# A bfloat16 column for the output tiles' scale, and ScalarE's square ahead of VectorE's product in the last tile

## The chip, the cores and the metric

The kernel runs on one core of a Trainium2 chip. The metric is the device time of one execution in microseconds (us), the median of several runs. The engines are named as in the profile: PE is TensorE (PEld its weight loads), DVE is VectorE, ACT is ScalarE, POOL is GpSimd, SP is SyncE, whose queue issues the transfers spoken of here.

## The reference

One decoder layer: a sequence of 2048 rows of 1024 features goes through two attention mixers (8 heads each, 64 wide), whose outputs are gated, put side by side, multiplied with the output weights, normalised and added to the input.

```python
def reference(x, c, positions, w_ada, b_ada, g_pre, w_in, b_fgate, sinks, w_out, g_post):
    ...
        h = rms_norm(x, g_pre[l]) * (1.0 + scale[:, None, :]) + shift[:, None, :]
        proj = h @ w_in[l]
        ...
        oa = oa * jax.nn.silu(za)
        ...
        ob = ob * jax.nn.silu(zb)
        y = jnp.concatenate([oa, ob], axis=-1) @ w_out[l]
        x = x + gate[:, None, :] * rms_norm(y, g_post[l])
```

`rms_norm(y, g)` divides each row by the root of its mean square (plus 1e-6) and multiplies by `g`. The change lies in the last two of these lines.

## The kernel before

All products run on PE in 16-bit floats: each f32 operand is scaled by a power of two or a similar factor into float16 range and split into a high and a low half, and a product is the sum of three matmuls (high by high, high by low, low by high). The program runs in stages: weights and input, the input projection with the sliding-window mixer, the forgetting attention (to about 1000 us), and then the output product, whose first tiles are mixed into the end of the attention.

**The output stage** goes over 16 tiles of 128 rows (class `Out`, `t` from 0 to 15). A tile passes these steps:

- `load`: SP's queue brings the attention outputs (`oT`, by transposing transfers, L1483; for the first four tiles `o`) and the gate path `z` (L1485).
- `turn`: the outputs are multiplied with `z` on DVE (`gate`, L1502 in tiles 0 to 3, L1505 and L1506 after them). ACT squares the product and sums along each row (`squares_`, L1510), which leaves one f32 number on each of the 128 partitions, the tile `gs` (shown as `w_mx`). `scale_` sums those 128 numbers over the partitions and gives every partition the sum: one PE matmul of the 128x128 matrix of ones (stationary) with the column `gs` (moving), L1514, into a PSUM column `pg`. `root_scale` (DVE, L128 and L129) makes from its bits an approximate reciprocal root `sc`, which scales the tile into float16 range; DVE also forms `inv`, with which the scale is taken out again later (L1518, L1519). ACT writes the high half of the scaled tile (`hi`, L1524), DVE the low half (`lo`, L1525); both make up `hl`, shown as `oz`.
- `product`: 48 matmuls over two halves of 512 output columns (L1576): per half, 8 units `k` of 3 matmuls each with 128x128 weights from `oz` and 512 columns of the output weights `wohl`. At the end of a half, DVE multiplies the PSUM result with `inv` and the gate row into `y` (L1585, shown as `hT`), and ACT squares the same PSUM result and sums it into `ss` (L1586, writes `sv`). `root` makes the reciprocal root of the mean square (L1596, then the small instructions L101 to L119), `store` the final multiply and add (L1605) and the transfer out (L1606).
- In the last tile (`t` = 15) the second half goes through `last`: two quarters of 256 columns (`h` = 0 and 1, 24 matmuls each, L1540), each with a product on DVE (L1547) and a square on ACT (L1548) of its own, so that after the very last matmul only a quarter's work is left. After `h` = 1 comes the reciprocal root on DVE (L103 to L119), then the final multiply and add in two halves (L1605), each followed by its transfer.

**What sets the order.** The stage is written out by hand: `ofill` calls the product units one after another, with the table `oev` naming the unit before which a tile's `load` or `turn` is called (`turn` of tile t comes 22 units before its first product). Work is put off by `after(n, f)`: `f` runs n ticks later; from tile 4 on a tick comes every second unit. `turn(5)` thus runs `gate` after 1 tick, the squares after 2, `scale_` after 5, `hi` after 6 and `lo` after 7. The instruction of `scale_` therefore sits between two product units of an earlier tile on PE's queue. Each engine takes its instructions in the order in which they were written, and waits on semaphores for those of other engines that wrote or read the same tile before.

Of the kernel before, what the change touches and what calls it, by code (L numbers as in the profile page):

```python
# [12 lines left out]
BF16 = mybir.dt.bfloat16  # L13
I16 = mybir.dt.int16
I32 = mybir.dt.int32
AF = mybir.ActivationFunctionType
# [27 lines left out]
def hybrid_layer(  # L44
# [17 lines left out]
    V, A, G, PE, SP = nc.vector, nc.scalar, nc.gpsimd, nc.tensor, nc.sync  # L62
# [20 lines left out]
    def sm(n, tag):  # L83
        return small.tile([P, n], F32, tag=tag, name=tag)
# [12 lines left out]
    def rsqrt_parts(dst, ss, n, more=None, eng=None):  # L97
        W = eng or V
        v = sm(n, "rs_v")
        if more is None:  # L100
            V.tensor_scalar(v[:], ss, 1.0 / D, EPS, op0=ALU.mult, op1=ALU.add)  # L101
        else:
            V.scalar_tensor_tensor(v[:], ss, 1.0 / D, more, op0=ALU.mult, op1=ALU.add)  # L103
        y = sm(n, "rs_y")
        h = small.tile([P, n], I32, tag="rs_h", name="rs_h")
        V.tensor_scalar(h[:], v[:].bitcast(I32), 1, None, op0=ALU.logical_shift_right)  # L106
        V.tensor_scalar(y[:].bitcast(I32), h[:], -1, 0x5F3759DF, op0=ALU.mult, op1=ALU.add)  # L107
        W.tensor_scalar(v[:], v[:], -0.5, None, op0=ALU.mult)
        for it in range(3):
            yield  # L110
            t = sm(n, "rs_t")
            if n == 1:
                W.scalar_tensor_tensor(t[:], y[:], y[:], v[:], op0=ALU.mult, op1=ALU.mult)  # L113
            else:
                W.tensor_tensor(t[:], y[:], y[:], op=ALU.mult)
                W.tensor_tensor(t[:], t[:], v[:], op=ALU.mult)
            y2 = dst if it == 2 else sm(n, "rs_y")
            if eng is None:
                V.scalar_tensor_tensor(y2[:], t[:], 1.5, y[:], op0=ALU.add, op1=ALU.mult)  # L119
            else:  # L120
                W.tensor_scalar(t[:], t[:], 1.5, None, op0=ALU.add)
                W.tensor_tensor(y2[:], t[:], y[:], op=ALU.mult)
            y = y2

    def root_scale(dst, ss):

        h = small.tile([P, 1], I32, tag="rs_h", name="sc_h")
        V.tensor_scalar(h[:], ss.bitcast(I32), 1, None, op0=ALU.logical_shift_right)  # L128
        V.tensor_scalar(dst.bitcast(I32), h[:], -1, 0x5F3759DF + (15 << 23), op0=ALU.mult, op1=ALU.add)  # L129
# [35 lines left out]
    ones = const.tile([P, P], F32, name="ones")  # L165
# [20 lines left out]
    def bank(hold=False):  # L186
        n = next(n for n in order_ if n not in held)
        order_.remove(n)
        order_.append(n)
        if hold:  # L190
            held.add(n)
        return n

    def release(n):
        held.discard(n)
        order_.remove(n)
        order_.append(n)
# [4 lines left out]
    def after(n, f):  # L202
        late.append([n, f])
# [227 lines left out]
    def turn(ci, k, px=None):  # L431

        px = px or ps_x.tile([P, CH], F32, tag="x", name="px")
        for u in range(4):
            PE.transpose(px[:, u * P:(u + 1) * P], xt[ci * 4 + u][:, k * P:(k + 1) * P], ident[:])
        hf = hst.tile([P, CH], F32, tag="hf", name="hf")
        hi, lo = hT[ci][:, 0, k, :], hT[ci][:, 1, k, :]

        def scaled():
            for dst in ([hi] if k % 2 == 0 else []) + [hf[:]]:  # L440
                A.activation(dst, px[:], AF.Identity, scale=Gp[:, k:k + 1], bias=Shp[:, k:k + 1])

        def split():
            if k % 2:
                V.tensor_copy(hi, hf[:])
            V.tensor_tensor(lo, hf[:], hi, op=ALU.subtract)

        return scaled, split

    def turn_x(ci, k):  # L450
        scaled, split = turn(ci, k)
        after(1, scaled)
        after(2, split)
# [9 lines left out]
    start = ExitStack()  # L463
    st = start.enter_context(tc.tile_pool(name="start", bufs=1, reuse_waits="tile"))
    wad = start.enter_context(tc.tile_pool(name="wad", bufs=8, reuse_waits="tile"))
    with tc.manual_schedule():
# [172 lines left out]
        w_low("kb", 0, 1)  # L639
        w_low("vb", 0, 1)  # L640
        turned = [turn(0, k) for k in range(5)]
        squares(1)
        shf0 = col8("shf0")
# [9 lines left out]

        PE.transpose(bk[0][0:1, 0:P], bmx[:], ident[:])
        turned += [turn(0, k, bk[k - 4]) for k in (5, 6)]
        bm = st.tile([1, 1], F32, name="bm")
        V.tensor_reduce(bm[:], bk[0][0:1, 0:P], axis=AX.X, op=ALU.max)
# [749 lines left out]
    def w_slot(n):  # L1407
        return oio["w"][:, n // KT, n % KT, :]
# [26 lines left out]
    def xy(n):  # L1435

        return hT[2][:, n // 2, 4 * (n % 2):4 * (n % 2) + 4, :].rearrange("p k n -> p (k n)").bitcast(F32)
# [24 lines left out]
    class Out:  # L1462
# [24 lines left out]
        def turn(self, lag):  # L1487

            if self.t < 4:
                px = [bk[bank()][:].rearrange("p (k n) -> p k n", k=4) for _ in range(2)]  # L1490
                for k in range(KT):
                    PE.transpose(px[k // 4][:, k % 4, :], self.o[:, k * P:(k + 1) * P], ident[:])
            self.hl = wpool.tile([P, 2, KT, P], F16, tag=("whl", "wraw")[self.t % 2], name="oz")
            self.sc = sm(1, "w_pw")
            hi, lo = self.hl[:, 0], self.hl[:, 1]
            gs = sm(1, "w_mx")

            def gate():
                if self.t < 4:
                    for h in range(2):  # L1500
                        z = self.z[:, 4 * h:4 * h + 4, :]
                        V.tensor_tensor(z, px[h], z, op=ALU.mult)  # L1502
                    return
                of = ozp.tile([P, KT, P], F32, tag="of", name="of")
                V.tensor_tensor(of[:], self.oT[:, 0], self.oT[:, 1], op=ALU.add)  # L1505
                V.tensor_tensor(self.z, of[:], self.z, op=ALU.mult)  # L1506

            def squares_():
                junk = stp.tile([P, KT, P], BF16, tag="st", name="zj")
                A.activation(junk[:], self.z, AF.Square, accum_out=gs[:])  # L1510

            def scale_():
                pg = bk[bank()][:, 0:1]
                PE.matmul(pg, ones[:], gs[:], start=True, stop=True)  # L1514
                root_scale(self.sc[:], pg)

                self.inv = sm(1, "w_sw")
                V.tensor_tensor(self.inv[:], self.sc[:], ysc[:], op=ALU.mult)  # L1518
                V.reciprocal(self.inv[:], self.inv[:])  # L1519

            after(1, gate)
            after(2, squares_)
            after(lag, scale_)
            after(lag + 1, lambda: A.activation(hi, self.z, AF.Copy, scale=self.sc[:]))  # L1524
            after(lag + 2, lambda: V.scalar_tensor_tensor(lo, self.z, self.sc[:], hi, op0=ALU.mult, op1=ALU.subtract))  # L1525

        def last(self, k):

            h, w = k // 4, CH // 2
            cc = slice(CH + h * w, CH + (h + 1) * w)  # L1530
            if k == 0:
                self.x = xy(self.t % 2)
                SP.dma_start(self.x[:], xs[self.t * P:(self.t + 1) * P, :])
            if k % 4 == 0:
                self.b = bank(True)
            b = self.b
            py = bk[b][:, 0:w]
            for k2 in range(2 * (k % 4), 2 * (k % 4) + 2):
                for m_, (i, j) in enumerate(((0, 0), (0, 1), (1, 0))):
                    PE.matmul(py, self.hl[:, i, k2, :], w_slot(8 * j + k2)[:, cc],  # L1540
                              start=(k2 == 0 and m_ == 0), stop=(k2 == KT - 1 and m_ == 2))
            if k % 4 < 3:
                return

            def evac():
                junk = stp.tile([P, 2, CH], BF16, tag="st", name="yj")
                V.scalar_tensor_tensor(self.y[:, cc], py, self.inv[:], gacc[:, cc], op0=ALU.mult, op1=ALU.mult)  # L1547
                A.activation(junk[:, 0, 0:w], py, AF.Square, scale=self.inv[:], accum_out=self.ss[:, 1 + h:2 + h])  # L1548
                release(b)
                if h == 0:  # L1550

                    self.more = sm(4, "a_ri")[:, 0:1]
                    V.tensor_tensor(self.more, self.ss[:, 0:1], self.ss[:, 1:2], op=ALU.add)
                    V.tensor_scalar(self.more, self.more, 1.0 / D, EPS, op0=ALU.mult, op1=ALU.add)
                else:
                    self.rst = sm(1, "y_rs")
                    for _ in rsqrt_parts(self.rst, self.ss[:, 2:3], 1, self.more):
                        pass
                    self.store()

            after(1, evac)

        def product(self, n, k):
# [220 lines left out]
```

## Time and profile before

| | |
|---|---|
| median of 3 runs | 1157.67 us (1157.06 to 1159.82) |
| the profiled execution, its own time | 1157.8 us |
| its span, first to last instruction | 1156.1 us |
| granted TensorE clock, mean | 0.996 |
| busy PE, DVE, ACT, POOL | 97%, 80%, 57%, 18% of the span |
| moved by DMA | 120.10 MB, mean 104 GB/s |

The profile is of one execution; its span is 1.7 us shorter than the time that this execution took. Engine rows give the busy share. A timeline row gives the start of an instruction in us from the start of the span, its duration, the engine, the line, the tiles written and read, and in brackets how long the engine was idle before it and for whom. Matmuls overlap, so the duration of one (0.38 us for 512 columns) is longer than the step from one start to the next; the ends of matmuls are modelled. A f32 matmul stands in the trace as two weight loads and two matmuls.

### The profile page before, as it was taken

To read this page: it belongs to the slowest core of one execution; us is meant where nothing else is said; L and a number is where in the kernel's file an instruction comes from. 1 tells how busy PE (TensorE), PEld (TensorE's weight loads), DVE (VectorE), ACT (ScalarE), POOL (GpSimd) and SP (SyncE) were. 2 spreads that over 40 slices of the span, in tenths; PEclk is the share of its full clock that TensorE was granted. 3 is DMA by queue.
4 is the path that set the end of the run, shared out by engine and by line. 5 is a ranking of instruction groups with operands and counts; after the bars stand their busy time and mean duration, and the time that the engine had idled before them with its cause. 6 is when DMAs were issued, how large, how long until landed. Compare 5 with 4: busy or idle time off the path is not lost. (4 is left out here: it accounts for less than half of the span.)

```text
span 1156.1 us, 25291 instructions
## 1 busy us (share of the span) xinstructions
PE 1116.8 (97%) x9869; PEld 656.3 (57%) x9869; DVE 930.5 (80%) x2137; ACT 661.4 (57%) x1150; POOL 207.5 (18%) x332
## 2 busy tenths in 40 slices
PE   5899999999999999999999999999999999999997
PEld 2475544577765866555555555555555555544444
DVE  7877468987888568788988899888888887878885
ACT  2876344654555421666757666666776778534332
POOL 1122134554556530010010110001000000000000
PEclk9899999999999999999999999999999999999999
DMA  9943355433243232442344342123311337686743
GB/s 333 336 116 72 87 78 96 97 63 90 52 92 88 58 87 58 73 108 29 80 64 87 84 67 70 38 49 76 45 43 34 91 101 206 140 225 197 199 135 109
DMA packets 123476, 120.10 MB, mean 104 GB/s; under 512 B 64948, under 2 KB 100828, under 8 KB 123356
## 3 DMA queue, kind: packets, MB, share of 16 engines
q1 hardware_dynamic: 112088, 85.69, 27.6%
q0 software_dynamic: 10832, 32.50, 13.5%
q8 instruction: 77, 1.26, 0.6%
q14 instruction: 43, 0.35, 0.1%
q10 hardware_dynamic: 436, 0.28, 0.1%
HBM read 64.75 MB, written 25.18 MB: 78 GB/s over the span
## 5 line engine op out<-in xcount | busy, mean ns | idle before, releaser
L1356 ACT ACTIVATE p<-sta,lift,scl_qk 128x1024 f32<-128x1024 f32 (+2 forms) x160 | 172.0, 1075 | 131.6 <-PE sta L1350 82.6
L351 PE MATMUL bk<-hT,wh_qk 128*128 128x512 f16 x768 | 194.7, 378 | 0.0
L1363 DVE TENSOR_TENSOR pha<-p,pha 128x1024 f16<-128x1024 f32 (+2 forms) x160 | 169.1, 1057 | 0.2 <-ACT pha L1360 0.2
L1303 DVE TENSOR_REDUCE a_m<-bk 128x1 f32<-128x512 f32 x192 | 130.4, 686 | 45.8 <-PE bk L1300 44.8
L1576 PE MATMUL bk<-wohl,oz 128*128 128x512 f16 x744 | 165.3, 379 | 1.1 <-DVE oz L1525 0.7
L1360 ACT ACTIVATE pha<-p 128x1024 f16<-128x1024 f32 (+2 forms) x160 | 148.1, 926 | 5.9 <-PE poa L1376 1.2
L1576 PEld LDWEIGHTS <-oz 128*128 128x128 f16 x744 | 71.9, 99 | 82.8 <-DVE oz L1525 1.8
L1376 PE MATMUL poa<-vt,pha 128*128 128x65 f16 x1088 | 116.1, 192 | 1.4 <-DVE pha L1363 1.2
L1373 PE MATMUL poa<-vt,pha 128*128 128x65 f16 x1088 | 116.6, 193 | 0.8 <-DVE ona L1382 0.7
L1375 PE MATMUL poa<-vt,pha 128*128 128x64 f16 x1088 | 116.6, 194 | 0.0
L351 PEld LDWEIGHTS <-wh_qk 128*128 128x128 f16 x768 | 72.1, 97 | 74.4 <-issue 2.1
L1349 PE MATMUL sta<-T 128*128 128x512 f16 (+1 forms) x320 | 110.9, 346 | 2.8 <-ACT p L1356 2.7
L1300 PE MATMUL bk<-T 66*128 66x512 f16 (+2 forms) x320 | 109.7, 348 | 2.4 <-DVE a_m L1303 1.9
L1373 PEld LDWEIGHTS <-pha 128*128 128x128 f16 x1088 | 101.5, 96 | 15.5 <-DVE ona L1382 1.9
L1350 PE MATMUL sta<-T 69*128 69x512 f16 (+1 forms) x320 | 109.8, 348 | 0.0
L1375 PEld LDWEIGHTS <-pha 128*128 128x128 f16 x1088 | 100.9, 97 | 11.4
L1376 PEld LDWEIGHTS <-pha 128*128 128x128 f16 x1088 | 100.8, 99 | 1.8 <-DVE pha L1363 1.7
L351 PE MATMUL bk<-hT,wh_za 128*128 128x512 f16 x384 | 99.7, 378 | 0.0
L369 PE MATMUL bk<-wh_va,hT 128*128 128x256 f16 x768 | 91.9, 273 | 0.0
L351 PE MATMUL bk<-hT,wh_zb 128*128 128x512 f16 x384 | 91.6, 379 | 0.2 <-DVE qc L754 0.2
L351 PE MATMUL bk<-hT,wh_qb 128*128 128x512 f16 x384 | 91.2, 379 | 0.0
L369 PEld LDWEIGHTS <-hT 128*128 128x128 f16 x768 | 73.3, 98 | 12.2 <-issue 2.1
(459 smaller groups left out, 1919.7 us busy)
## 6 DMA issues: line engine op xcount, KB each, us to landing
hT<-in_x_dram SPq DMA_DIRECT2D x20, 512.0 KB
wa<-in_w_ada_dram SPq DMA_DIRECT2D x16, 512.0 KB
z_d<-tz POOLq DMA_DIRECT2D x32, 256.0 KB, 3.0
T<-z_d SPq DMA_DIRECT2D x16, 512.0 KB
T<-stq SPq DMA_DIRECT2D x62, 128.0 KB
out_dram<-hT SPq DMA_DIRECT2D x15, 512.0 KB
xt<-in_x_dram SPq DMA_DIRECT2D x12, 512.0 KB
qs<-qf SPq DMA_DIRECT2D x80, 64.0 KB
```

What stands on the lines that cost most here:

```text
L351: PE.matmul(ps, whl[:, a, k, :], hT[ci][:, b, k, :], start=(k == 0 and n == 0), stop=(k == KT - 1 and n == 2))
L369: PE.matmul(ps[:, (u % 2) * 2 * P:(u % 2 + 1) * 2 * P], hT[ci][:, a, k, u * P:(u + 1) * P], wv[p][:, b, k, :], start=(k == 0 and n == 0), ...
L1303: V.tensor_reduce(m3[:, u, pc:pc + 1], mx[:, :w], axis=AX.X, op=ALU.max)
L1349: PE.matmul(self.st[:, o:o + w], T[:, 3, kb_], T[:, 1, qc], start=True, stop=False)
L1350: PE.matmul(self.st[:, o:o + w], T[0:XR, 2, kb_], T[0:XR, 0, qc], start=False, stop=not diag)
L1356: A.activation(self.p32[:, :self.w], self.st[:, :self.w], AF.Exp, scale=scl[f"qk{self.hd}"][:], bias=lift[:])
L1360: A.activation(self.ph[:, 0, :self.w], self.p32[:, :self.w], AF.Copy)
L1363: V.tensor_tensor(self.ph[:, 1, :self.w], self.p32[:, :self.w], self.ph[:, 0, :self.w], op=ALU.subtract)
L1373: PE.matmul(po[:, u, :], ph[:, 0, pq], vt[:, b, hd, 0:65], start=(self.first and n == 0 and u == 0), stop=False)
L1375: PE.matmul(po[:, u, 0:64], ph[:, 0, pq], vt[:, b, hd, 65:VW], start=False, stop=False)
L1376: PE.matmul(po[:, u, :], ph[:, 1, pq], vt[:, b, hd, 0:65], start=False, stop=(self.last and n == len(self.blocks) - 1))
L1576: PE.matmul(py, self.hl[:, i, k, :], w_slot(8 * j + k)[:, cc], start=(k == 0 and m_ == 0), stop=(k == KT - 1 and m_ == 2))
```

## The change

Two edits in the class `Out`. In `scale_`, the operands of the spreading matmul are read as bfloat16: of each f32 number only the upper 16 bits, which are a bfloat16 number by themselves. For the ones that is every second 16-bit element of the tile `ones` (exactly 1.0), for the sums the second of the two 16-bit halves of each `gs`, so each sum enters the product cut off to bfloat16; `inv` is made from the same `sc`, so the scale still cancels. In `last`, ACT's square is written ahead of DVE's product.

```diff
@@ turn @@
             gs = sm(1, "w_mx")
+            gs1 = gs[:].bitcast(BF16)[:, 1:2]
...
             def scale_():
                 pg = bk[bank()][:, 0:1]
-                PE.matmul(pg, ones[:], gs[:], start=True, stop=True)
+                PE.matmul(pg, ones[:].bitcast(BF16).rearrange("p (n two) -> p two n", two=2)[:, 1], gs1,
+                          start=True, stop=True)
                 root_scale(self.sc[:], pg)
@@ last @@
             def evac():
                 junk = stp.tile([P, 2, CH], BF16, tag="st", name="yj")
+                A.activation(junk[:, 0, 0:w], py, AF.Square, scale=self.inv[:], accum_out=self.ss[:, 1 + h:2 + h])
                 V.scalar_tensor_tensor(self.y[:, cc], py, self.inv[:], gacc[:, cc], op0=ALU.mult, op1=ALU.mult)
-                A.activation(junk[:, 0, 0:w], py, AF.Square, scale=self.inv[:], accum_out=self.ss[:, 1 + h:2 + h])
                 release(b)
```

The lines after the edits move: L1514 becomes L1515, L1547 (product) becomes L1550, L1548 (square) becomes L1549, L1576 becomes L1578, L1585 and L1586 become L1587 and L1588. SP's and POOL's queues hold the same instructions in the same order.

On PE's queue, in the middle of a product of the output stage, the spreading matmul stands between two product units. Names: `oz` is the scaled tile, `wohl` the output weights, `w_mx` the sums, `bk` a PSUM bank. Before:

```order
L1576 LDWEIGHTS oz
L1576 MATMUL bk_138<-wohl,oz 128x512
L1514 MATMUL bk_137<-w_mx,ones 128x1 [waits Activation_49]
L1576 LDWEIGHTS oz
L1576 MATMUL bk_138<-wohl,oz 128x512
```

and now:

```order
L1578 LDWEIGHTS oz
L1578 MATMUL bk_138<-wohl,oz 128x512
L1515 LDWEIGHTS ones
L1515 MATMUL bk_137<-w_mx,ones 128x1 [waits Activation_49]
L1578 LDWEIGHTS oz
L1578 MATMUL bk_138<-wohl,oz 128x512
```

The weight load of the ones has become an instruction of its own, without a wait; the matmul behind it keeps the wait for ACT. This holds for all 16 tiles; no other row of PE's queue moves.

On ACT's queue, its last rows, the end of the last two tiles (`y_ss` takes the sums of squares, `w_sw` is `inv`). Before:

```order
L1586 ACTIVATE sv,y_ss<-bk_138,w_sw 128x512 [waits DVE_49,Activation_49]
L1586 ACTIVATE sv,y_ss<-bk_6031,w_sw 128x512 [waits DVE_49,Activation_49]
L1586 ACTIVATE sv,y_ss<-bk_6030,w_sw 128x512 [waits DVE_49,Activation_49]
L1548 ACTIVATE sv,y_ss<-bk_136,w_sw 128x256 [waits DVE_49,Activation_49]
L1548 ACTIVATE sv,y_ss<-bk_137,w_sw 128x256 [waits DVE_49,Activation_49]
```

and now:

```order
L1588 ACTIVATE sv,y_ss<-bk_138,w_sw 128x512 [waits DVE_49,Activation_49]
L1588 ACTIVATE sv,y_ss<-bk_6031,w_sw 128x512 [waits DVE_49,Activation_49]
L1588 ACTIVATE sv,y_ss<-bk_6030,w_sw 128x512 [waits DVE_49,Activation_49]
L1549 ACTIVATE sv,y_ss<-bk_136,w_sw 128x256 [waits PE_49,Activation_49]
L1549 ACTIVATE sv,y_ss<-bk_137,w_sw 128x256 [waits PE_49,Activation_49]
```

The two squares of the last tile's quarters wait for PE where they waited for DVE; the other squares still wait for DVE.

On DVE's queue at the same place, from the last full product to the start of the last reciprocal root (`gacc` is the gate row, `a_ri` a sum carried from the first quarter to the second). Before:

```order
L1605 SCALAR_TENSOR_TENSOR hT_109<-hT_109,y_rs 128x1024 [waits DMAHW6_49,DVE_49]
L1547 SCALAR_TENSOR_TENSOR hT_109<-bk_136,w_sw,gacc 128x256 [waits PE_49]
L1553 TENSOR_TENSOR a_ri<-y_ss 128x1 [waits Activation_49]
L1554 TENSOR_SCALAR a_ri<-a_ri 128x1 [waits DVE_49]
L1547 SCALAR_TENSOR_TENSOR hT_109<-bk_137,w_sw,gacc 128x256 [waits PE_49]
L103 SCALAR_TENSOR_TENSOR rs_v<-y_ss,a_ri 128x1 [waits Activation_49]
```

and now:

```order
L1607 SCALAR_TENSOR_TENSOR hT_109<-hT_109,y_rs 128x1024 [waits DMAHW6_49,DVE_49]
L1550 SCALAR_TENSOR_TENSOR hT_109<-bk_136,w_sw,gacc 128x256 [waits Activation_49]
L1555 TENSOR_TENSOR a_ri<-y_ss 128x1
L1556 TENSOR_SCALAR a_ri<-a_ri 128x1 [waits DVE_49]
L1550 SCALAR_TENSOR_TENSOR hT_109<-bk_137,w_sw,gacc 128x256 [waits Activation_49]
L103 SCALAR_TENSOR_TENSOR rs_v<-y_ss,a_ri 128x1 [waits DVE_49]
```

The two products now wait for ACT, the two readers of the sums no longer do; the order of DVE's rows is the same.

## The prediction

> **What bounds the kernel now.** I read the engine shares first, then the chain of work that ended last, then the stretch in which the changed instructions stand.
>
> ```profile
> PE 1116.8 (97%) x9869; PEld 656.3 (57%) x9869; DVE 930.5 (80%) x2137; ACT 661.4 (57%) x1150; POOL 207.5 (18%) x332
> PE 12%; DVE 0%; DVEq 0%; ACT 0%; issue 0%; ACTq 0%
> 1066.27 0.12 PE bk L1514 x2
> 1066.38 10.38 PE bk L1576 x48
> 1076.77 0.12 PE bk L1514 x2
> 1142.98 5.25 PE bk L1540 x48
> 1148.26 0.50 DVE hT L1547
> ```
>
> The first row is the page's first part, the second the heading of its chain, the others pieces of the chain (start, length, what). The chain goes back only to about 1010 us, and there it is PE alone, 12% of the span, until DVE takes over at 1148.26. In each output tile 48 product matmuls follow each other without a hole, and one spreading product (x2: two passes) lies among them, on the path. The shares by stretch say the same:
>
> ```profile
> 1000.00:1012.10 12.10, 11.96 (x60) 5.70 (x59) 11.10 (x27) 4.53 (x8) 0.00 (x0) 1.00 0.99 205
> 1012.10:1142.70 130.60, 130.60 (x622) 61.23 (x623) 102.58 (x262) 45.89 (x84) 0.00 (x0) 1.00 0.64 182
> L1514 PE MATMUL bk<-w_mx,ones 128*128 128x1 f32 x24 | 3.3, 208 | 0.0
> ```
>
> The columns are the stretch, its length, then busy us of PE, PEld, DVE, ACT and POOL, the granted clock and the DMA share; the third row is the group view of the second stretch. From 1012.1 to 1142.7 us PE is busy all 130.60 us at clock 1.00, so a nanosecond taken from PE's queue there is a nanosecond off the end. Of the 16 spreading products 12 (24 records) stand in it, one per tile from tile 4 on. Nothing else binds: DVE works 102.58 us, ACT 45.89, and the operand made from the spread sum is never waited for here: in the waits of this stretch no PE row appears.
>
> **The spreading product, what it costs now.** The busy time of 3.3 us is no price, since matmuls overlap. I take it from starts:
>
> ```profile
> 1066.11 0.28 PE L1514 MATMUL bk<-w_mx,ones 128*128 128x1 f32 x2
> 1066.13 0.25 PE L1514 MATMUL bk<-w_mx,ones 128*128 128x1 f32 x1
> 1066.24 10.52 PE L1576 MATMUL bk<-wohl,oz 128*128 128x512 f16 x48
> 1076.74 10.52 PE L1576 MATMUL bk<-wohl,oz 128*128 128x512 f16 x48
> 1129.22 13.76 PE L1576 MATMUL bk<-wohl,oz 128*128 128x512 f16 x63
> 1142.82 5.40 PE L1540 MATMUL bk<-wohl,oz 128*128 128x256 f16 x48
> ```
>
> A tile's period is 1076.74 − 1066.24 = 10.50 us. The step of an undisturbed product is (1142.82 − 1129.22) / 63 = 0.216 us, 48 of them 10.36. The rest, **0.14 us**, is the spreading product: its first pass starts at 1066.11, its second about 0.03 later (the row 1066.13 is that pass alone), and the next product 0.11 after that, at 1066.24. So the dear part is not a pass over one column but the 0.11 us in which the next weights come in behind a f32 pass.
>
> **What it costs then.** One pass and one 16-bit weight load. The load of the ones has no wait and lies under the 0.216 us of the product in front. No 16-bit matmul of one column is in the trace. The nearest rows are the attention's short ones, each with a 128x128 float16 weight load of its own:
>
> ```profile
> 701.03 0.19 PE L1373 MATMUL poa<-vt,pha 128*128 128x65 f16 x1
> 701.06 0.19 PE L1375 MATMUL poa<-vt,pha 128*128 128x64 f16 x1
> ...
> 701.73 0.19 PE L1376 MATMUL poa<-vt,pha 128*128 128x65 f16 x1
> 701.76 0.38 PE L351 MATMUL bk<-hT,wh_za 128*128 128x512 f16 x1
> 958.32 1.07 PE L1492 MATMUL bk<-ident,T 128*128 128x128 f32 x8
> ```
>
> 24 matmuls run from 701.03 to 701.76, one in 0.030 us, and the product of 512 columns behind them also follows after 0.03. The f32 transposes in the last row are the contrast: eight in 1.07 us, the last still counted with its whole duration, so about 0.11 each for 128 columns. Bounds for the new price: nothing (a product wholly absorbed, saving 0.14), and 0.11 (the following load stays as slow as it is behind a f32 pass, saving 0.03). I take 0.03 since the load behind it is one of 16-bit weights behind a 16-bit pass, as in the attention's rows: **0.11 us saved per tile, 12 × 0.11 = 1.3 us** (bounds 0.36 and 1.7).
>
> The Trainium skill says otherwise in "TensorE: Matmul & The Clock Gate", section "Back-to-back issue gap": a sustained pair of weight load and matmul takes about 81 ns at 128 columns. By that figure the saving would be an estimated 0.06 us a tile, 0.7 us in all. This trace has 0.030 us for such pairs, so I do not use it, but the result may lie between.
>
> **The four earlier spreading products** stand in front of 1012.1 us, the first at 955.78, the third at 988.55. Behind these PE waits for work that ACT feeds, so what it saves is waited away:
>
> ```profile
> 955.78 0.28 PE L1514 MATMUL bk<-w_mx,ones 128*128 128x1 f32 x2
> 956.72 0.38 PE L1349 MATMUL sta<-T 128*128 128x512 f16 x1 [0.66 <-ACT p L1356]
> 988.55 0.28 PE L1514 MATMUL bk<-w_mx,ones 128*128 128x1 f32 x2
> 999.52 0.20 PE L1376 MATMUL poa<-vt,pha 128*128 128x65 f16 x1 [0.61 <-DVE pha L1363]
> ```
>
> The brackets tell how long PE was idle and for whom. Both waits are for exponentials of the attention, which no changed instruction feeds, and the second lies behind all of the first three. I count these at nothing; if that cover were gone, 3 × 0.11 = 0.3 us more would be gained. The fourth is different:
>
> ```profile
> 1006.59 0.30 PEld L1514 LDWEIGHTS bk<-w_mx,ones 128*128 128x128 f32 x2 [0.48 <-ACT sv L1510]
> 1006.59 0.38 PE L1514 MATMUL bk<-w_mx,ones 128*128 128x1 f32 x2
> 1007.01 0.16 DVE L128 TENSOR_SCALAR sc_h<-bk 128x1 int32<-128x1 int32 x1 [0.46 <-PE bk L1514]
> 1009.62 1.23 DVE L1506 TENSOR_TENSOR T<-of,T 128x1024 f32<-128x1024 f32 x1
> 1010.76 1.28 DVE L1525 SCALAR_TENSOR_TENSOR oz<-T,w_pw,oz 128x1024 f16<-128x1024 f32 x1
> 1012.10 0.33 PEld L1576 LDWEIGHTS <-oz 128*128 128x128 f16 x3 [0.63 <-DVE oz L1525]
> ```
>
> Here the f32 instruction waits for ACT with its weight load, both loads and both passes come after the wait, and DVE gets the sum 0.42 us after 1006.59. From there DVE works almost without a hole until it has written `oz` at 1012.04, for which PE waits. With the ones loaded beforehand, one pass is left behind the wait: the short matmuls above take 0.19 us, and DVE would start about 0.04 later, at 1006.82, 0.19 us earlier. What is late next is the transfer of `z` and of the outputs, in a stretch with a DMA share of 0.99; so I take **0.15 us**, bounds 0 and 0.19.
>
> **The last tile.** The end of the program now:
>
> ```profile
> 1143.02 0.75 DVE L1585 SCALAR_TENSOR_TENSOR hT<-bk,w_sw,gacc 128x512 f32<-128x512 f32 x1 [1.39 <-PE bk L1576]
> 1143.69 1.28 DVE L1605 SCALAR_TENSOR_TENSOR hT<-hT,y_rs 128x1024 f32<-128x1024 f32 x1
> 1146.82 0.16 DVE L1553 TENSOR_TENSOR a_ri<-y_ss 128x1 f32<-128x1 f32 x1 [0.69 <-ACT sv L1548]
> 1148.26 0.48 DVE L1547 SCALAR_TENSOR_TENSOR hT<-bk,w_sw,gacc 128x256 f32<-128x256 f32 x1 [1.10 <-PE bk L1540]
> 1148.84 0.47 ACT L1548 ACTIVATE sv<-bk,w_sw 128x256 bf16<-128x256 f32 x1 [2.06 <-DVE hT L1547]
> 1149.21 0.19 ACT L1548 ACTIVATION_READ_ACCUMULATOR sv<-bk,w_sw 128x1 f32 x1
> 1149.44 0.16 DVE L103 SCALAR_TENSOR_TENSOR rs_v<-y_ss,a_ri 128x1 f32<-128x1 f32 x1 [0.69 <-ACT sv L1548]
> ```
>
> PE ends at 1142.82 + 5.40 = 1148.22. DVE's product, then ACT's square, then DVE's root run one behind the other: the root starts 1.22 us after PE. Product and square only read the same PSUM, yet each is kept behind the other by a wait, and the change turns this round; it does not make them run beside each other. Then: ACT starts 0.04 after PE, as DVE does now, or 0.10, as ACT now does behind DVE (1148.74 to 1148.84); DVE can go on 0.60 after ACT's start (1148.84 to 1149.44); the root starts behind the 0.48 us product on the same engine, where consecutive DVE instructions overlap by 0.08 (a product of 0.75 at 1143.02, its dependent at 1143.69), so 0.40 on. Sum 1.04 to 1.10, a gain of 0.12 to 0.18; I take **0.15 us**. Bounds: 0.02 if the overlap fails and the late ACT start holds; 0.18. The work behind is as before: root, two halves of L1605, the transfers out. In the first quarter the new wait holds up only the sums `a_ri` behind it on DVE. These end at 1147.2 now, 1.1 us before DVE is next needed, which hides a shift of that size.
>
> **Sum:** 1.3 + 0.15 + 0.15 = 1.6 us, so the profiled execution of 1157.8 us (span 1156.1, 1.7 around it) would become 1156.2; it lies 0.1 above the median of 1157.67, which becomes **1156.1 us**.
>
> **The rivals.**
>
> *The load behind the narrow pass stays slow.* What costs 0.11 us now may be the exchange of weights behind a pass too short to hide it, whatever the type. For it: the 0.11 stands behind a pass of one column. Against it: the attention's 64 columns are as short in effect and step at 0.030. Price: 12 × 0.03 + 0.3 = 0.66 us saved, 1157.0 us. The page's 81 ns would give 1.0 saved, an estimate of 1156.7.
>
> *More comes through than I count.* The narrow pass vanishes under its neighbours, the three early products come through, and the fourth and the end give their upper bounds: 1.7 + 3 × 0.14 + 0.2 + 0.2 = 2.5 us, 1155.2. Against it stand the waits at 956.72 and 999.52 us, and that no start in the rows above follows another by less than 0.03.
>
> *The strided ones load slowly: slower than before.* The new weights are read as every second 16-bit element, a pattern that no row shows. Place: the load in front of each spreading product. It stays free up to the 0.216 us of the product before it, and from 0.216 + 0.14 − 0.03 = 0.33 us it costs more than the change gains per tile. The f32 loads of the ones bound it from the other end:
>
> ```profile
> 1065.89 0.41 PEld L1514 LDWEIGHTS bk<-w_mx,ones 128*128 128x128 f32 x2
> ```
>
> Two in succession take 0.41 us, one about 0.2, so the strided one would have to take 1.65 times that. At twice, 0.41 us, PE loses 0.08 × 12 = 1.0 us against before, with 0.3 regained at the other places: 1158.4; at three times, 0.62 us, 0.29 × 12 − 0.3 = 3.2 us, 1160.9.
>
> The Trainium skill speaks against this rival: in the same page, section "Weight-path perf modes", the fast load needs 128 weights that are not FP32 and a column step within about a thousand elements, which a step of two meets. The row of the attention's loads agrees for packed weights; for strided ones no run shows it.
>
> *The change does not do what it says* in one respect: square and product do not overlap (above). That is in the sum.
>
> **How the numbers follow.** Forecast 0.72 (1155.6 to 1156.6 by its bounds), slow following load or the gap between 0.13, more gained 0.08, slower 0.07. Repeated runs of before lay between 1157.06 and 1159.82, so the median of a few can sit some tenths off, rather above than below. The range 1154.6 to 1158.2 takes in the first three cases, the mild end of the fourth and such a shift. A measurement of this kernel tells about 0.3% (3.5 us) from no change. All cases but the fourth's far end lie inside that: within 0.3% 0.88; faster by more 0.08, which needs a gain that I have not found, since even the upper bounds add up to 2.5; slower by more 0.04.
>
> **What would show it.** In the changed profile: one record of the spreading product per tile, the next product 0.03 us behind it, and a period of 10.39 us. The span from the first product of tile 4's second pass at 1012 us to the last matmul shortens by 1.3 us. At the fourth turn DVE follows ACT's sum by about 0.23 us, not 0.42. At the end ACT starts before DVE and the root starts 1.04 to 1.10 us behind PE. A period of 10.47 speaks for the slow load, one above 10.50 for the strided ones. I am wrong if the time moves by more than the 2.5 us that all places together hold, for then something changed that these rows do not contain.

## The result and the profile after

| | before | changed |
|---|---|---|
| median of 10 runs each | 1157.96 us (1156.62 to 1159.82) | 1154.75 us (1153.44 to 1156.25) |
| ratio, 95% interval | | 0.9972 (0.9962 to 0.9982) |
| the profiled execution, its own time | 1157.8 us | 1156.25 us |
| its span | 1156.1 us | 1154.5 us |

The change is faster, by 0.28%, which is about the 0.3% named as the bound. The two traces differ by 1.6 us of span, the medians by 3.2 us; two more measurements of the same pair (below) gave 0.9985 and 0.9984, 1.9 and 1.7 us by the medians. One execution of the changed kernel in the first of these two, the one that was profiled there, took 2523.82 us, more than twice the others, and is left out of the ratio.

First the changed kernel's PE in the output stage, from its timeline (start, duration, engine, line, tiles):

```profile
1065.47 0.17 PE L1515 MATMUL bk<-w_mx,ones 128*128 128x1 bf16 x1
1065.50 10.52 PE L1578 MATMUL bk<-wohl,oz 128*128 128x512 f16 x48
1075.86 0.17 PE L1515 MATMUL bk<-w_mx,ones 128*128 128x1 bf16 x1
1075.89 10.52 PE L1578 MATMUL bk<-wohl,oz 128*128 128x512 f16 x48
```

One record of the spreading product per tile, the next product 0.03 us behind it, a period of 1075.89 − 1065.50 = 10.39 us against 10.50. The 0.14 us have become 0.03. The stretch behind the fourth turn, in shares (as before: PE, PEld, DVE, ACT, POOL, clock, DMA share, GB/s):

```profile
1012.10:1141.30 129.20, 129.20 (x610) 58.71 (x611) 102.53 (x262) 45.88 (x84) 0.00 (x0) 1.00 0.65 181
```

PE is still busy without a hole, at the full granted clock, and still the bound; the stretch is simply shorter. The fourth turn, the changed kernel's timeline, with ACT's sum as it stood before in the first fence:

```profile
1006.36 0.19 ACT L1510 ACTIVATION_READ_ACCUMULATOR sv<-T 128x1 f32 x1
```

```profile
1006.36 0.10 PEld L1515 LDWEIGHTS <-ones 128*128 128x128 bf16 x1
1006.49 0.19 ACT L1511 ACTIVATION_READ_ACCUMULATOR sv<-T 128x1 f32 x1
1006.73 0.16 PE L1515 MATMUL bk<-w_mx,ones 128*128 128x1 bf16 x1
1006.93 0.16 DVE L128 TENSOR_SCALAR sc_h<-bk 128x1 int32<-128x1 int32 x1 [0.24 <-PE bk L1515]
1009.55 1.23 DVE L1507 TENSOR_TENSOR T<-of,T 128x1024 f32<-128x1024 f32 x1
1012.02 0.11 PEld L1578 LDWEIGHTS <-oz 128*128 128x128 f16 x2 [0.64 <-DVE oz L1527]
```

The load of the ones now lies ahead of the wait (1006.36, while ACT is still summing). DVE starts 1006.93 − 1006.68 = 0.25 us behind ACT's sum; before it was 1007.01 − 1006.55 = 0.46. All of these 0.21 us arrive: from DVE's first instruction to the next gate product it is 2.62 us, as before (2.61), and PE's restart moves with it. Last the end of the program:

```profile
1141.41 5.40 PE L1542 MATMUL bk<-wohl,oz 128*128 128x256 f16 x48
1146.91 0.47 ACT L1549 ACTIVATE sv<-bk,w_sw 128x256 bf16<-128x256 f32 x1 [2.06 <-PE bk L1542]
1147.28 0.19 ACT L1549 ACTIVATION_READ_ACCUMULATOR sv<-bk,w_sw 128x1 f32 x1
1147.51 0.48 DVE L1550 SCALAR_TENSOR_TENSOR hT<-bk,w_sw,gacc 128x256 f32<-128x256 f32 x1 [1.88 <-ACT sv L1549]
1147.91 0.15 DVE L103 SCALAR_TENSOR_TENSOR rs_v<-y_ss,a_ri 128x1 f32<-128x1 f32 x1
```

ACT starts first, 0.10 us after PE's end at 1146.81, DVE 0.60 after ACT, the root 0.40 after DVE: 1.10 us behind PE, against 1.22.

**Where the time went.** The two traces are set against each other at the same instructions, the spread sum's first reader on DVE (L128), once per tile. The first of them:

```profile
956.09 0.16 DVE L128 TENSOR_SCALAR sc_h<-bk 128x1 int32<-128x1 int32 x1
```

in before, and

```profile
956.31 0.16 DVE L128 TENSOR_SCALAR sc_h<-bk 128x1 int32<-128x1 int32 x1
```

in the changed kernel. From there to the end of the span it is 1156.08 − 956.09 = 199.99 us before and 1154.53 − 956.31 = 198.22 now:

| from, to | before | changed | difference |
|---|---|---|---|
| first sum to that of tile 3 (fourth turn) | 50.92 | 50.62 | −0.30 |
| to that of tile 4 | 6.93 | 6.85 | −0.08 |
| to that of tile 15 (11 tiles) | 115.46 | 114.24 | −1.22 |
| to the end of the last matmul | 18.82 | 18.79 | −0.03 |
| to the last root's start | 1.22 | 1.10 | −0.12 |
| to the end | 6.64 | 6.62 | −0.02 |
| sum | 199.99 | 198.22 | −1.77 |

What the first spreading product gains lies ahead of these two rows, so the table leaves it out. Counted from the end of ACT's first sum, up to which both programs have the same instructions, it is in. That sum in before

```profile
955.38 0.19 ACT L1510 ACTIVATION_READ_ACCUMULATOR sv<-T 128x1 f32 x1
```

and in the changed kernel:

```profile
955.68 0.19 ACT L1511 ACTIVATION_READ_ACCUMULATOR sv<-T 128x1 f32 x1
```

From its end to the end of the span it is 1156.08 − 955.57 = 200.51 us before and 1154.53 − 955.87 = 198.66 now, 1.85 us less. Up to it the changed kernel's trace is 0.30 us later, with the same instructions. So this pair of traces has the gain at the places of the change, and not more.

### The profile page after: what moved, and what is told of

It is laid out like the page before. It is cut to its first block, busy times and chain, and to the rows that moved or that the text cites. A ratio compares the mean times of both kernels' runs of the same rounds, so it can differ in the third digit from the quotient of the medians.

```text
span 1154.5 us, 25258 instructions
## 1 busy us (share of the span) xinstructions
PE 1116.1 (97%) x9853; PEld 654.1 (57%) x9853; DVE 929.8 (81%) x2137; ACT 661.2 (57%) x1150; POOL 208.8 (18%) x332
## 5 line engine op out<-in xcount | busy, mean ns | idle before, releaser
L1363 DVE TENSOR_TENSOR pha<-p,pha 128x1024 f16<-128x1024 f32 (+2 forms) x160 | 169.2, 1058 | 0.2 <-ACT pha L1360 0.2
L1578 PE MATMUL bk<-wohl,oz 128*128 128x512 f16 x744 | 163.7, 379 | 1.1 <-DVE oz L1527 0.7
L1578 PEld LDWEIGHTS <-oz 128*128 128x128 f16 x744 | 70.6, 98 | 84.7 <-DVE oz L1527 1.8
```

The lines of the kernel that those rows point to most:

```text
L1363: V.tensor_tensor(self.ph[:, 1, :self.w], self.p32[:, :self.w], self.ph[:, 0, :self.w], op=ALU.subtract)
L1578: PE.matmul(py, self.hl[:, i, k, :], w_slot(8 * j + k)[:, cc], start=(k == 0 and m_ == 0), stop=(k == KT - 1 and m_ == 2))
```

## The experiments

Two theories stood at the start. A: the edits are worth what their places show, 1.8 us, and the rest of the 3.2 us is scatter of the part that both programs share. B: they are worth all of it. The first four kernels were measured beside 33 runs of before (median 1156.97 us, 1154.94 to 1158.13). Where no time is given below, the kernel was executed once, and only its trace is read.

**The kernel before against itself.** No edit.

> The kernel before, unchanged, measured against itself: ratio 1.000, and its scatter from run to run. Theory A (the two edits are worth what their places show, 1.8 us in the profiled run, and the rest of the measured 3.2 us is scatter of the part of the program that both kernels share): single runs scatter by 2 us or more and the trace differs from the first trace of before by up to 1 us ahead of 950 us. Theory B (the edits are worth the whole 3.2 us): the traces of the same kernel agree within 0.3 us at 950 us.

1156.97 us (1155.80 to 1158.13), ratio 1.0001 (0.9993 to 1.0010). The first spread sum:

```profile
955.82 0.16 DVE L128 TENSOR_SCALAR sc_h<-bk 128x1 int32<-128x1 int32 x1
```

From there to the end of its span (1155.81) it is 199.99 us, the same as in the first trace to a hundredth. The executions of one kernel scatter by 2.3 us; these two traces differ by 0.27 us ahead of the first sum, and by nothing behind it. That alone fits both theories; the next run decides.

**The changed kernel once more.** No edit.

> The changed kernel, unchanged, measured once more. Theory A: 1.8 us below before, ratio 0.9984, with the whole gain behind 955 us of the trace: 0.11 a tile over 12 tiles, 0.2 to 0.3 at the fourth turn, 0.12 at the end. Theory B: 3.2 us below, ratio 0.9972 again, and the trace shows about 1.4 us of it ahead of 955 us, where the instructions are the same.

1155.06 us, ratio 0.9985 (0.9976 to 0.9994): 1.9 us, as A says. No trace of this measurement is used; where in the program the gain lies is read from the third one, at the end of this section.

**Only the bfloat16 product.**

The first edit of the diff alone; `last` is that of the kernel before.

```diff
+            gs1 = gs[:].bitcast(BF16)[:, 1:2]
...
-                PE.matmul(pg, ones[:], gs[:], start=True, stop=True)
+                PE.matmul(pg, ones[:].bitcast(BF16).rearrange("p (n two) -> p two n", two=2)[:, 1], gs1,
+                          start=True, stop=True)
```

> Only the bfloat16 product, the last tile as before. Theory A: 1.7 us below before (12 x 0.11 and 0.25 to 0.4 at the four early turns), ratio 0.9985; the root of the last tile starts 1.22 us behind PE as before. Theory B: about 3.0 us below.

1155.02 us, ratio 0.9989 (0.9980 to 0.9998). First sum and end in the trace:

```profile
954.93 0.16 DVE L128 TENSOR_SCALAR sc_h<-bk 128x1 int32<-128x1 int32 x1
1140.04 5.40 PE L1542 MATMUL bk<-wohl,oz 128*128 128x256 f16 x48
1146.66 0.16 DVE L103 SCALAR_TENSOR_TENSOR rs_v<-y_ss,a_ri 128x1 f32<-128x1 f32 x1 [0.69 <-ACT sv L1550]
```

With a span of 1153.31 us, 198.38 us from the first sum to the end, 1.61 below before; PE ends at 1140.04 + 5.40 = 1145.44, and the root starts 1.22 behind it, as before.

**Only the exchange in the last tile.** The diff's second edit alone, with the f32 product.

```diff
+                A.activation(junk[:, 0, 0:w], py, AF.Square, scale=self.inv[:], accum_out=self.ss[:, 1 + h:2 + h])
                 V.scalar_tensor_tensor(self.y[:, cc], py, self.inv[:], gacc[:, cc], op0=ALU.mult, op1=ALU.mult)
-                A.activation(junk[:, 0, 0:w], py, AF.Square, scale=self.inv[:], accum_out=self.ss[:, 1 + h:2 + h])
```

> Only the exchange in the last tile, the product in f32. Theory A: 0.12 us below before, too little to be told in the time (ratio 0.9999), but seen in the trace: the root starts 1.10 us behind PE and not 1.22. Theory B, in the form that the exchange brings the unexplained part: 1.4 to 1.5 us below.

1156.90 us, ratio 1.0003 (0.9994 to 1.0011): not to be told in the time. The trace:

```profile
955.33 0.16 DVE L128 TENSOR_SCALAR sc_h<-bk 128x1 int32<-128x1 int32 x1
1142.07 5.40 PE L1540 MATMUL bk<-wohl,oz 128*128 128x256 f16 x48
1147.57 0.47 ACT L1547 ACTIVATE sv<-bk,w_sw 128x256 bf16<-128x256 f32 x1 [2.06 <-PE bk L1540]
1148.16 0.48 DVE L1548 SCALAR_TENSOR_TENSOR hT<-bk,w_sw,gacc 128x256 f32<-128x256 f32 x1 [1.88 <-ACT sv L1547]
1148.57 0.15 DVE L103 SCALAR_TENSOR_TENSOR rs_v<-y_ss,a_ri 128x1 f32<-128x1 f32 x1
```

PE ends at 1142.07 + 5.40 = 1147.47, the root starts 1.10 behind it; from the first sum to the end of the span (1155.18) it is 199.86 (of unrounded times), 0.13 below before. The two edits add up: 1.61 + 0.13 = 1.74, against 1.77 with both.

**Why the f32 product cost 0.14: the product twice.** In the kernel before, the line of the spreading matmul stands twice:

```diff
                 PE.matmul(pg, ones[:], gs[:], start=True, stop=True)
+                PE.matmul(pg, ones[:], gs[:], start=True, stop=True)
```

> The kernel before with the f32 spreading product issued twice in a row into the same column. If the 0.11 us is the load of the next weights behind every f32 matmul (theory A), the second costs as much as the first: period 10.50 + 0.14 = 10.64 us, 1.7 us longer over 12 tiles. If it is one exchange from f32 to 16-bit weights, however many f32 passes stand before it (theory C), the second adds only two passes: 0.06 us a tile, period 10.56, 0.7 us in all.

1161.27 us, beside 10 runs of before with a median of 1157.54; ratio 1.0026 (1.0015 to 1.0038), 3.0 us slower by it, more than either theory said. The period says where:

```profile
1068.02 0.28 PE L1514 MATMUL bk<-w_mx,ones 128*128 128x1 f32 x2
1068.16 0.36 PE L1515 MATMUL bk<-w_mx,ones 128*128 128x1 f32 x2
1068.38 10.52 PE L1577 MATMUL bk<-wohl,oz 128*128 128x512 f16 x48
1078.74 0.28 PE L1514 MATMUL bk<-w_mx,ones 128*128 128x1 f32 x2
```

10.72 us from 1068.02 to 1078.74. The second product starts 0.14 after the first, as expected, but the next one in 16 bits 0.22 after that: the two passes of the second product are 0.11 apart (in the first pair 0.03), and 0.11 more pass before the 16-bit product. The weight loads of the four passes tell why:

```profile
1067.80 0.41 PEld L1514 LDWEIGHTS bk<-w_mx,ones 128*128 128x128 f32 x2
1068.13 0.30 PEld L1515 LDWEIGHTS bk<-w_mx,ones 128*128 128x128 f32 x2
```

One record is 0.19 long. So the four start at 1067.80, 1068.02, 1068.13 and 1068.24: the first under the long product in front, the second with the first pass, the others 0.11 apart. A load of f32 weights holds up what comes behind it by 0.11 us, and a matmul can follow its own load by 0.03. The first load's 0.11 lies under the 0.216 us of the product in front; the other three are paid for: 0.03 + 3 × 0.11 = 0.36, the distance from 1068.02 to 1068.38. In the kernel before it is one load, the pair's second: 0.03 + 0.11 = 0.14. At its fourth turn, where both loads come after the wait for ACT, the second pass starts 0.13 behind the first and not 0.03 (0.38 for the two from 1006.59 on, of which the second alone takes 0.25). This is read from the starts of the records; what PE does in the 0.11 us no run shows.

**The bfloat16 product twice.** The same in the changed kernel.

> The changed kernel with the bfloat16 spreading product issued twice in a row. Theory A (a narrow 16-bit pass costs its step of 0.03 us and leaves nothing slow behind it): period 10.39 + 0.03 = 10.42 us. Theory D (two passes in a row are what makes the load behind them slow, whatever the type): period 10.50 as with f32.

```profile
1065.37 0.17 PE L1515 MATMUL bk<-w_mx,ones 128*128 128x1 bf16 x1
1065.39 0.16 PE L1517 MATMUL bk<-w_mx,ones 128*128 128x1 bf16 x1
1065.42 10.52 PE L1580 MATMUL bk<-wohl,oz 128*128 128x512 f16 x48
1075.78 0.17 PE L1515 MATMUL bk<-w_mx,ones 128*128 128x1 bf16 x1
```

A period of 10.41: the second narrow pass with its own load costs 0.03 us and leaves nothing slow behind it. Two passes in a row are not what is dear; their type is.

**f32 and bfloat16 one behind the other.** In the changed kernel:

```diff
+                PE.matmul(pg, ones[:], gs[:], start=True, stop=True)
                 PE.matmul(pg, ones[:].bitcast(BF16).rearrange("p (n two) -> p two n", two=2)[:, 1], gs1,
                           start=True, stop=True)
```

> The changed kernel with the f32 product in front of the bfloat16 one, both into the same column. Theory A (the load right behind a f32 pass takes 0.11 us, the one behind a 16-bit pass 0.03): steps 0.03 (f32 to f32), 0.11 (to bfloat16), 0.03 (to the product), period 10.36 + 0.17 = 10.53 us. Theory E (once f32 weights have been loaded, every load is slow until a long product hides one): steps 0.03, 0.11, 0.11, period 10.61 us.

```profile
1066.62 0.28 PE L1515 MATMUL bk<-w_mx,ones 128*128 128x1 f32 x2
1066.76 0.16 PE L1516 MATMUL bk<-w_mx,ones 128*128 128x1 bf16 x1
1066.79 10.52 PE L1579 MATMUL bk<-wohl,oz 128*128 128x512 f16 x48
1077.14 0.28 PE L1515 MATMUL bk<-w_mx,ones 128*128 128x1 f32 x2
```

The load in front of the bfloat16 pass:

```profile
1066.65 0.18 PEld L1516 LDWEIGHTS <-ones 128*128 128x128 bf16 x1
```

The bfloat16 pass follows the f32 pair after 0.14 (0.03 and 0.11), the 16-bit product follows the bfloat16 pass after 0.03; period 10.52. Theory A holds and E does not: the 16-bit load right behind a f32 load is held up for 0.11 (its record is 0.18 long, where that of the changed kernel is 0.10), the one behind that is not. With the double f32 product this says that the dear thing is the f32 load, whatever type is loaded next.

**Packed ones.** In the changed kernel, the first half of `ones` is written over when the output stage opens (a packed tile of their own does not fit: the pool `wsp` needs 2 kb per partition, and 1.875 would be left):

```diff
+        V.memset(ones[:].bitcast(BF16)[:, 0:P], 1.0)
...
-                PE.matmul(pg, ones[:].bitcast(BF16).rearrange("p (n two) -> p two n", two=2)[:, 1], gs1,
-                          start=True, stop=True)
+                PE.matmul(pg, ones[:].bitcast(BF16)[:, 0:P], gs1, start=True, stop=True)
```

> The changed kernel with packed ones: when the output stage opens, the first half of the tile of ones is written over with 128 packed bfloat16 ones (one small VectorE instruction more), and the spreading product takes its weights from there. Theory A (strided weights load as fast as packed ones, or their load is hidden): period 10.39 us and weight load records of about 0.10 us, as with the strided ones. If strided loading costs anything on the path: a period below 10.39, at least 10.36.

The load records of the packed ones (ns, least, median and most):

```profile
L1516 PEld LDWEIGHTS <-ones x16: 97/98/98, 954.6 to 1126.4; 128*128 128x128 bf16 x16
```

and of the strided ones of the changed kernel:

```profile
L1515 PEld LDWEIGHTS <-ones x16: 97/98/98, 955.9 to 1127.6; 128*128 128x128 bf16 x16
```

They are alike, and the period is 10.39 with both. No cost of the stride is seen.

**No spreading at all.** The product is left out and the scale made from each partition's own sum.

```diff
-                pg = bk[bank()][:, 0:1]
-                PE.matmul(pg, ones[:].bitcast(BF16).rearrange("p (n two) -> p two n", two=2)[:, 1], gs1,
-                          start=True, stop=True)
-                root_scale(self.sc[:], pg)
+                bank()
+                root_scale(self.sc[:], gs[:])
```

> The changed kernel without the spreading product: each partition takes the scale from its own sum, the sum over partitions is left out. It shows what is left to gain at this place. Theory A: period 10.36 us (48 steps of 0.216), 0.03 us a tile and 0.3 to 0.4 us over 12 tiles below the changed kernel, and about 0.25 us more at the fourth turn, where DVE then follows ACT directly.

```profile
1061.71 26.49 PE L1576 MATMUL bk<-wohl,oz 128*128 128x512 f16 x122
```

122 products without a break, (26.49 − 0.38) / 121 = 0.216 us a step, 10.36 us a tile. From the first reader of a sum (955.67) to the end of the span (1153.40) it is 197.73 us, 0.49 below the changed kernel, a little less than the 0.55 to 0.65 that were expected. That is all that is left at this place.

**The square first in every tile.** In the changed kernel, the same exchange in `product`:

```diff
+                A.activation(junk[:, 0, :], py, AF.Square, scale=self.inv[:], accum_out=self.ss[:, n:n + 1])
                 V.scalar_tensor_tensor(self.y[:, cc], py, self.inv[:], gacc[:, cc], op0=ALU.mult, op1=ALU.mult)
-                A.activation(junk[:, 0, :], py, AF.Square, scale=self.inv[:], accum_out=self.ss[:, n:n + 1])
```

> The changed kernel with ScalarE's square ahead of VectorE's product in all tiles, not only in the last. Theory A (away from the end the order of the two is hidden by TensorE): period 10.39 us, ratio to the changed kernel 1.000, the end as in the changed kernel. Rival: VectorE, which waits for ScalarE behind each half tile, takes some 0.6 us a half longer, uses up its 2 us of slack a tile and delays the scaled tile for TensorE: a period above 10.39 and TensorE waiting for the scaled tile.

1157.01 us, 0.9997 (0.9988 to 1.0006) of before: by the medians the whole gain is gone again. In its trace, from the first sum (956.28) to the end of the span (1155.74), 0.5 us of it are left: 199.47 against 199.99 before and 198.22 in the changed kernel. The rival was right about DVE, and the wait came up at another place than it named. The waits from 1012 us on (us in all, times, longest), and turns of the timeline, of PE and then of DVE:

```profile
DVE hT L1588 <- ACT sv L1587: 12.7, 14, 2.4
```

```profile
1065.92 0.17 PE L1515 MATMUL bk<-w_mx,ones 128*128 128x1 bf16 x1
1076.30 0.17 PE L1515 MATMUL bk<-w_mx,ones 128*128 128x1 bf16 x1
1118.45 0.16 PE L1515 MATMUL bk<-w_mx,ones 128*128 128x1 bf16 x1
1128.77 0.18 ACT L1511 ACTIVATION_READ_ACCUMULATOR sv<-T 128x1 f32 x1
1129.01 0.16 PE L1515 MATMUL bk<-w_mx,ones 128*128 128x1 bf16 x1
```

```profile
1067.00 0.15 DVE L128 TENSOR_SCALAR sc_h<-bk 128x1 int32<-128x1 int32 x1
1077.55 0.15 DVE L128 TENSOR_SCALAR sc_h<-bk 128x1 int32<-128x1 int32 x1
```

At 1066 us PE's period is still 10.38, but DVE already takes 10.55 from tile to tile. DVE, waiting for ACT's squares, falls behind by these 0.17 us a tile, with it the gate product and ACT's sum of it, until PE itself waits at the spreading product: it starts 0.06 behind ACT's sum at 1128.95, and the period is 1129.01 − 1118.45 = 10.56, more than with the f32 product. So the exchange, worth 0.12 us in the last tile, costs more than that when it stands in every tile.

**The changed kernel a third time.** No edit.

> The changed kernel once more, since two measurements of it against before gave 0.9972 and 0.9985. Theory A (1.9 us): ratio 0.9984, and from the first spreading sum to the end 198.2 us in the trace against 200.0 in the traces of before. Theory B (3.2 us): ratio 0.9972.

1155.33 us against 1157.06 (21 runs), ratio 0.9984 (0.9975 to 0.9993).

```profile
955.19 0.16 DVE L128 TENSOR_SCALAR sc_h<-bk 128x1 int32<-128x1 int32 x1
```

With a span of 1153.43 us it is 198.24 us from there to the end, as in the first trace (198.22). Theory A again.

## Why the prediction was right

**The spreading product on PE, 1.3 us.** Right in mechanism and size. The step fell from 0.14 to 0.03, and from the fourth turn to the last matmul the tables show 0.08 + 1.22 + 0.03 = 1.33 us. The reason given, that the next weights come in late behind a f32 pass, is what the runs show: 0.11 behind f32, 0.03 behind bfloat16, with one pass or two. They add whose time it is: that of the f32 load in front, the pair's second, and not of the load that is late.

The Trainium skill's 81 ns in "TensorE: Matmul & The Clock Gate", section "Back-to-back issue gap", is a figure for 128 columns. The changed kernel's pair has one column and steps at 0.03 us, as the attention's pairs of 64 and 65 columns do; pairs of 128 columns in the trace of before start 0.05 to 0.06 us apart (700.80, 700.86, 700.91, 700.97), so the figure does not hold there either.

**The fourth turn, 0.15 us.** Undersized: 0.21. The step worked out 0.19 and then took some off since the transfers might be late next, in a stretch with a DMA share of 0.99. Nothing was late: the work behind the sum keeps its pace to 0.01 us. The 0.42 that the prediction gives for DVE behind ACT's sum counts from PE's load at 1006.59; from the end of the sum at 1006.55 it was 0.46.

**The three early turns, nothing.** Wrong: half came through. From the end of ACT's first sum to the end of its sum at the fourth turn it is 1006.55 − 955.57 = 50.98 before and 1006.68 − 955.87 = 50.81 now, 0.17 us of the 0.33 that they could have brought. The wait at 956.72 hid what the first turn saved, as argued. The wait at 999.52 did not hide the others: in the changed trace it is as long as before,

```profile
999.65 0.20 PE L1376 MATMUL poa<-vt,pha 128*128 128x65 f16 x1 [0.61 <-DVE pha L1363]
```

and ends 999.65 − 955.87 = 43.78 us behind ACT's first sum, where it was 999.52 − 955.57 = 43.95. So the operand came earlier too. The step that failed is the one that no changed instruction feeds this wait: DVE writes the operand (`pha`, L1363), and in before DVE stood idle for the third spreading product some 10 us ahead of it,

```profile
988.87 0.16 DVE L128 TENSOR_SCALAR sc_h<-bk 128x1 int32<-128x1 int32 x1 [1.00 <-PE bk L1514]
```

so a sum that comes earlier lets DVE's later work start earlier. Between the two DVE waits only once more, 1.5 us for PE's output product, which moved as well.

**The last tile, 0.15 us.** 0.12, the lower end of the stated 0.12 to 0.18. ACT started 0.10 behind PE and not 0.04; the two following steps, 0.60 and 0.40, came as worked out. (The rows from which the overlap of 0.08 was taken are not a product and its dependent: the one at 1143.02 belongs to the last tile, the one at 1143.69 to the tile before. The root does not read the product either, so the step fits.)

**The sum.** 1.6 us was forecast; the traces show 1.77 from the first sum's reader on and 1.85 from ACT's first sum on, the two later measurements 1.9 and 1.7. What is over comes from the early turns (0.17) and the fourth (0.06 more). That the expected 1156.2 us for a profiled execution met 1156.25 is luck in part: the changed trace is 0.30 us later ahead of ACT's first sum, which takes back what the places brought beyond the forecast. The forecast's band of 1155.6 to 1156.6 follows the bounds only at its lower end; the smallest savings add up to 0.36 + 0 + 0.02, which is 1157.3.

The median of 1154.75 lies 1.4 us below the forecast and only 0.15 above the lower end of the range. The 3.2 us between the medians are also more than the 2.5 us that the prediction named as its sign of being wrong; taken alone, the first comparison speaks against it, and only the repeats and the traces bear it out. What the medians show beyond the traces is not in the places of the change: behind the first sum all traces of before agree at 199.99, and those of the changed kernel at 198.22 and 198.24. What is left is the part ahead of the first sum, which ends between 954.93 and 956.31 us in the traces quoted here, with no order between the kernels, and the scatter of single executions (2.3 us for one kernel). Why the first comparison drew 3.2 us, with an interval that ends at 0.9982, was not settled; the point estimates of both repeats lie just above it.

**The rivals.** A slow load behind the narrow pass: no, 0.03. More gained than counted: only the 0.17 and 0.06 above. Slow strided loads: no, the records are those of packed ones, as the Trainium skill's section "Weight-path perf modes" in "TensorE: Matmul & The Clock Gate" lets expect. And square and product did not overlap, as said.

## What to carry to other kernels

A f32 matmul of one column between long 16-bit ones cost 0.14 us here, 0.11 of it by the second of its two weight loads, which nothing hides: read the steps from start to start around it, and where the sum may be cut off to 16 bits because the factor cancels later, take the upper halves of the f32 numbers in place; no cost of the stride was seen. When two engines that read the same result are kept one behind the other, the exchange of their order was worth something here only at the end of the program; in every tile it put a wait on the bounding engine some tiles later. A wait hides a saving only if what it waits for does not come earlier by the same saving: follow the queue of the engine that feeds it. And an effect of 0.15% is better told by the distance between two instructions of the trace, which repeats here to 0.02 us, than by the medians, which moved by more than 1 us from one comparison to the next.

## What was not expected

The second f32 product in a row costs 0.22 us where the first costs 0.14: its first load is no longer hidden. And ACT, released by PE, started its square 0.10 us after PE's end, where DVE, released by PE at the same place before, started 0.04 after it; the prediction had left open which it would be. The order of rows shows that the square waits for two semaphores and the product for one. In the chain of the changed trace that ended last, the square's wait for PE is a row of its own on ACT's queue (start, length), and the square starts 0.06 behind it, at 1146.91:

```profile
1146.85 0.02 ACTq L1549
```
